# Bias strips from a table of ready rows, and new transfer estimates for a list scheduler, in a hybrid decoder step

## The chip, the core and the metric

The kernel runs on one core of one Trainium2 chip. The metric is the device time of one execution in microseconds. The time before is the median of three runs, 277.95 us (275.93, 277.95 and 278.9). A separate execution was profiled; its page and its trace are what is read here.

## The reference

One layer of a decoder trunk, for a new prompt of 512 tokens and for eight sequences that each add one token to a past. One projection of the 1024 wide input gives nine groups of columns; two mixers use them, and an output projection, a residual and a layer norm follow.

```python
h = jnp.einsum('btd,de->bte', x, w_in)
qa, ka, va, za, ga, qb, kb, vb, gb = jnp.split(h, split_points, axis=-1)
# mixer A: gated linear attention, 4 heads, dk 64, dv 128
log_a = jax.nn.log_sigmoid(einsum('btr,rk->btk', za, w_alpha2) + b_alpha) / 16
o_a, s_new = gla_chunked(qa * DK_A**-0.5, ka, va, log_a, s0, chunk=64)
o_a = o_a * rsqrt(mean(o_a**2) + eps) * gla_norm_g
# mixer B: 8 heads of 64; three (window, dilation) patterns: (128,1), (512,4), (2048,16)
logits = einsum('bqhd,bqjhd->bhqj', q, kg) * scale + rel_bias[t5_bucket(dist)]
# softmax over each pattern; the three outputs merged by their denominators
mix = concatenate([o_a * silu(ga), o_b * silu(gb)])
x_new = layer_norm(DEEPNORM_ALPHA * x + mix @ w_out, ln_g, ln_b)
```

Outputs are the new rows of the prompt and of the samples, both recurrent states, and the keys and values of both. All inputs and outputs are float32.

The three patterns share keys, so for a prompt the kernel adds them up: a key at distance d counts as often as patterns hold it, and the logarithm of that count is part of the bias. The bias depends on the distance alone. It is added to a tile of scores in which partition p holds the query p of a block and the columns hold keys; along the partitions the same sequence of biases is therefore shifted.

## The kernel before

Every product of the projections is made in three passes of fp32r (`three`): inputs and weights are split into a high and a low part, and hi x hi, lo x hi and hi x lo are added in PSUM. A feature group of 128 columns (`feature`) takes two banks of the class `d`, one for each half of the tokens (264 and 256 columns), with 24 matmuls each; after each an evacuation task is added that reads the bank on the vector engine (DVE) and the scalar engine (ACT). There are eight PSUM banks: three `d`, three `s`, two `t`.

Weights arrive as 512 KB transfers, are split by ACT (cast to the high part) and DVE (difference, the low part), and are taken in the fixed order of `ORDER`. The tasks of mixer A (levels `ps_l`, the diagonal `near`, the state), of mixer B and of the sample path run beside that.

Mixer B of a prompt goes by `scores(m, pi)`: m is one of four pairs of heads, pi one of two halves of the queries, so there are eight blocks. One block makes the scores of two heads and two query tiles in a batch of matmuls (`ps_s`). Then comes `softmax` for each head and tile: DVE adds the bias strip and takes the row extreme in one custom instruction (`tensor_tensor_reduce`, printed as ISA in the orders and as CUSTOM_DVE_ANT_0 in the trace) with a readout behind it; ACT takes the exponential with its sum; DVE inverts the sum; DVE or ACT scales; for the dilated part DVE transposes blocks of 32; PE transposes the probabilities (`ps_pt`), and DVE or ACT copies them to SBUF. `weighted` multiplies them with the values.

A **strip** is the bias tile of one head and one half: 128 partitions with 256 columns (pi = 0) or 320 (pi = 1). `bias_table` computes 768 biases for each of the 8 heads by two matmuls, writes them to DRAM (`tab`) and copies them within DRAM to `tabr`, where each of the 8 rows stands 35 times. Because a row is 768 long, a read with a step of 767 or 764 in place of 768 gives the shifted rows. `strips` reads each strip from there with an access pattern of 4 x 32 rows of 256; for pi = 1 a second transfer reads 64 more columns.

The **order of the work** is set by a planner (`Plan`). Every task is a generator that hands out its next instruction. Each step takes, over all tasks, the instruction that can begin earliest by estimated times, and among equals the lower priority number; matmuls of ordinary tasks count as ready only `SPARE` ns after their inputs. The order found is the program's order on each engine (PE, DVE, ACT, GpSimd as POOL, SyncE as SP, which issues nearly all transfers); on the chip each engine works strictly in that order. A step that gives two choices (`V.tensor_scalar(...), S.mul(...)`, or `copy`) takes the engine that would end first by the estimates. So the estimates decide the order and which engine copies, while the chip's own times decide how long it takes. The estimate of a transfer is in `Op.__init__`: bytes by a rate that is chosen from the run length and the outermost count, plus 600 ns for one class. A priority is the second argument of `add`.

All instructions are issued by one helper, so nearly every row of the profile has the line L377; rows are told apart by the names of their tiles.

Of the kernel before, what the change touches and what calls it, by code (L numbers as in the profile page):

```python
# [11 lines left out]
F32 = mybir.dt.float32  # L12
# [8 lines left out]
P = 128  # L21
# [9 lines left out]
HA, HB = 4, 8  # L31
# [23 lines left out]

T_N = 512
T_P = 768
T_R = 35
T_D = T_N + 128
T_W = T_D + 258  # L60

N_WARM = 7
ROWS = 66

SLOTS = dict(
    g=23,
    w=8, r=3,
    sv=4,
    pt=2, far=5, tp=2, vp=2,
    t2=2, st=3,  # L70
    pr=4,
    t1=5, ob=3,
    m=6)
BANKS = dict(d=3, s=3, t=2)


# [3 lines left out]
SWITCH = 140  # L80
RING = 8
PIECE = 256
SPARE = 800.0

ORDER = "qa0 qb0 qb1 qb2 qb3 kb0 kb1 vb0 kb2 kb3 gb0 vb1 gb1 gb2 va0 gb3 va1 ga0 ga1 ga2 ga3".split()

# [1 line left out]
class Op:  # L88
# [3 lines left out]
    def __init__(self, eng, fn, args, kw):  # L92
        self.eng, self.fn, self.args, self.kw = eng, fn, args, kw
        Op.made += 1
        aps = [x for x in args if isinstance(x, bass.AP)]
        extra = [x for x in kw.values() if isinstance(x, bass.AP)]
        self.writes, self.reads = [aps[0]], aps[1:] + [x for k, x in kw.items() if isinstance(x, bass.AP) and k != "accum_out"]
        if "accum_out" in kw:
            self.writes.append(kw["accum_out"])
        if fn == "tensor_tensor_reduce":  # L100
            self.writes.append(self.reads.pop())
        n = max(size(x) for x in aps + extra)
        psum = any(x.tensor.space == bass.MemoryType.PSUM for x in aps)
        self.mode = None
        self.port = eng.name == "POOL" or (eng.name == "DVE" and len(aps) + len(extra) > 1 and not psum and n > 64)
        if fn == "dma_start":
            c = 640 if eng.name == "SP" else 100
            x = aps[aps[0].tensor.space == bass.MemoryType.DRAM]
            run = 4 * min(run_of(x) for x in aps)

            rate = 130 if run <= 128 else 175 if x.ap[0][1] <= 64 else 340 if run >= 4096 else 230
            self.xfer = max(4 * total(x) / rate, 200)
            self.late = 600 * (rate == 175)
        elif eng.name == "PE":
            m, n, slow = size(aps[1]), size(aps[2]), aps[2].dtype == F32

            self.mode = tuple(32 if x <= 32 else 64 if x <= 64 else P for x in (aps[1].ap[0][1], m if slow and fn != "transpose" else P))
            r0 = aps[1].offset // aps[1].ap[0][0] // 32
            c0 = aps[0].offset // aps[0].ap[0][0] // 32 if self.mode[1] < P else 0
            self.cells = [(r, k) for r in range(r0, r0 + self.mode[0] // 32) for k in range(c0, c0 + self.mode[1] // 32)]  # L120
            self.gap = 17 if slow and fn != "transpose" else 5
            if fn == "transpose":
                c = 109
            else:
                c = 2 * max(n * .8333 + 2, m * .83 + 5) if slow else max(n, 64) * .4167 + 11
        elif eng.name == "DVE":
            fast = fn in ("tensor_copy", "tensor_scalar", "memset") and not psum
            ptr = fn in ("tensor_scalar", "scalar_tensor_tensor") and any(size(x) == 1 for x in aps[1:]) and n > 1
            c = ((n / 2 if fast else n) + (155 if fn == "transpose" else 124 if ptr else 66)) / .96
        elif eng.name == "ACT":  # L130
            c = n / 1.2 + (52 if psum else 97) + 90 * (len(extra) + (fn == "mul" and len(aps) > 2))
        else:
            c = n * .87 if fn == "memset" else n * 2.15 + 100
        self.cost = c


def run_of(x):

    n = 1
    for step, c in reversed(x.ap[1:]):  # L140
        if step != n:
            break
        n *= c
    return n


def size(x):
# [234 lines left out]
def trunk(ctx: ExitStack, tc: tile.TileContext, xT, xp, xs, state, ck, cv, w_in, wab, gnorm,  # L382
# [78 lines left out]
    o_pv, o_bs, o_as = cst("o_pv", [P, 4, NB]), vnt, cst("o_as", [P, NB * HA])  # L461
    yts = lt[:, 0, :].rearrange("p (m b) -> p m b", b=NB)
    ga_s, gb_s = cst("ga_s", [P, 4, NB]), cst("gb_s", [P, 4, NB])
    tabr = dram.tile([HB, T_R, T_P], F32, name="tabr")
    vad = dram.tile([NB, 512], F32, name="vad")
    qsd = dram.tile([NB, 512], F32, name="qsd")
    psd_s = dram.tile([64, 256], F32, name="psd_s")
# [215 lines left out]
    def feature(g, evac):  # L683

        yield At(g.name)
        for u in range(2):
            ps = yield bank("d", f"ps_{g.name}{u}")
            for k in range(KT):
                yield from three(ps[:, :TW[u]], k, halves(k, u, g))
            add(evac(ps, u), 2)  # L690
        g.done(0)

    def token(g, evac_f, evac):
# [87 lines left out]
    def dense():  # L781
# [25 lines left out]
                             start=k == 0, stop=k == KT - 1, skip_group_check=True)  # L807
                    for k in range(KT) for j in range(TT))
        free(zw, *xraw)
        add(gate_decay(pz), 24.7)  # L810
        yield from make("ka", Need("g", "ka", [P, 2, NP]), 3)
        yield from make("qa", Need("g", "qa", [P, 2, NP]), 2)
        for n in first:
# [62 lines left out]

    def bias_table():
        yield At("const")
        tab = dram.tile([HB, T_P], F32, name="tab")
        raw = yield Need("g", "ct_raw", [66, T_D])  # L880
        yield D.dma_start(raw, c_t[:, :T_D])
        ct = yield Need("g", "ct", [66, T_D], F32R)
        yield V.tensor_copy(ct, raw)
        free(raw)
        tsb = yield Need("g", "tsb", [HB, T_P])
        yield V.memset(tsb[:, T_N:T_P - P], NEG)
        yield At("rb")
        for c, to in ((slice(0, T_N), slice(0, T_N)), (slice(T_N, T_D), slice(T_P - P, T_P))):
            pt = yield bank("t", "ps_tab")
            yield T.matmul(pt[:HB, :c.stop - c.start], rb[:, 0, :], ct[:, c], start=True, stop=True)  # L890
            yield copy(tsb[:, to], pt[:HB, :c.stop - c.start])
            free(pt)
        yield D.dma_start(tab, tsb)
        free(ct, tsb)
        yield D.dma_start(tabr, tab[:, None, :].to_broadcast([HB, T_R, T_P]))
        mark("tab")


# [326 lines left out]
    def strips():  # L1225
        yield At("tab")
        yield At("qb", 1)
        for h0, pi in ((0, 0), (0, 1), (4, 0), (4, 1)):
            for h in range(h0, h0 + 4):
                yield At(f"kb{h // 2}{pi}")  # L1230
                strip = yield Need("st", f"strip{h}{pi}", [P, 256 + 64 * pi])
                plan.share(strip, 2)
                B["strip", h, pi] = strip
                row = tabr[h]
                yield D.dma_start(strip[:, 64 * pi:], bass.AP(tensor=row.tensor, offset=row.offset + T_N - P - 1, ap=[[T_P - 1, 4], [T_P - 4, 32], [1, 256]]))
                if pi:
                    yield D.dma_start(strip[:, :64], bass.AP(tensor=row.tensor, offset=row.offset + T_P - P + 31, ap=[[0, 4], [T_P - 1, 32], [1, 64]]))
                mark(f"strip{h}{pi}")

    def scores(m, pi):  # L1240
# [26 lines left out]
        for v in range(2):  # L1267
# [1 line left out]
                plan.share(ps[v, qt[0]], 2)  # L1269
                plan.share(pr[v, qt[0]], 2)  # L1270
            for q in qt:
                add(softmax(2 * m + v, q, ps[v, q], pr[v, q], cols[q]), 31 + m // 2 / 5 + pi / 10 + m % 2 / 50)

    def softmax(h, q, ps_all, pr_all, cols):
        ps, pr = ps_all[:, cols], pr_all[:, cols]
# [583 lines left out]
    add(sample_values(), 14.3)  # L1859
    add(sample_v(vnt, "vnt", by_tile(vw_s)), 21.3)  # L1860
    add(sample_v(vat, "vat", by_tile(vad)), 21.3)
    add(sample_past(), 19.3)
    add(sample_state(), 61)
    add(sample_gla(), 24.7)
    add(mix_sample_a(), 20.7)
    add(mix_sample_b(), 12.3)
    add(ln_rows(), 19.3)
# [5 lines left out]
    for pi in range(2):  # L1873
        for n in "ab":
            add(mix_tiles(n, pi), 12.7)
        for m in range(4):
            add(scores(m, pi), 31 + m // 2 / 5 + pi / 10 + m % 2 / 50)
        for g in range(2):
            add(weighted(g, pi), 30 + g / 5 + pi / 10)
        for j in range(2):  # L1880
# [104 lines left out]
```

## Time and profile before

| what | value |
| --- | --- |
| three timed runs | 275.93, 277.95, 278.9 us |
| span of the profiled execution | 275.6 us (its own time beside the span is not given) |
| PE busy | 266.9 us, 97%, 2881 instructions |
| DVE busy | 214.6 us, 78% |
| ACT busy | 158.5 us, 58% |
| POOL busy | 52.8 us, 19% |
| DMA | 52.58 MB, mean 191 GB/s |
| packets under 512 B | 13645 of 61527 |

The page gives each engine's busy time, the chain of work that ended last and the costliest groups. The waits of an engine list what it stood idle for and what released it. A table of windows gives the same by stretch. The timeline gives single instructions with their start and duration.

### The profile page before, as it was taken

What the parts mean: (1) busy time and instruction counts of PE and PEld (TensorE: products, weight loads), DVE (VectorE), ACT (ScalarE), POOL (GpSimd) and SP (SyncE); (2) the same over time, 40 slices, a digit from 0 to 9 for tenths busy, and PEclk for the clock granted to TensorE, in tenths of its full rate; (3) what the DMA queues carried; (4) which work ended last, traced back from release to release, by engine and by line L of the source; (5) the groups of instructions that cost most, each with busy time, mean ns of one, the idle gap of its engine ahead of it and who ended that gap; (6) DMA issues with size and microseconds to landing.
All of it is one profiled execution on the core that took longest, in us unless ns stands there. A gap on an engine that the chain in (4) does not pass through costs nothing.

```text
span 275.6 us, 7460 instructions
## 1 busy us (share of the span) xinstructions
PE 266.9 (97%) x2881; PEld 252.1 (91%) x2881; DVE 214.6 (78%) x578; ACT 158.5 (58%) x478; POOL 52.8 (19%) x71
## 2 busy tenths in 40 slices
PE   8999999999899999999999999999999999999990
PEld 5999999999899989989999999999999999998890
DVE  4845899998989497998396963738999999239984
ACT  4727886475538583877686824535668886224401
POOL 3000000000534260703000633744242000000000
PEclk9999999999999999999999999999999999999998
DMA  7977939436967898556497979893897660980432
GB/s 219 340 181 190 266 91 235 125 104 179 311 188 161 243 291 276 157 115 157 87 258 195 221 202 188 250 279 92 265 246 194 179 223 6 293 239 0 180 129 76
DMA packets 61527, 52.58 MB, mean 191 GB/s; under 512 B 13645, under 2 KB 53715, under 8 KB 61493
## 3 DMA queue, kind: packets, MB, share of 16 engines
q1 hardware_dynamic: 60917, 51.66, 67.2%
q8 instruction: 22, 0.36, 0.5%
q10 hardware_dynamic: 576, 0.46, 0.5%
q14 instruction: 12, 0.10, 0.1%
HBM read 46.02 MB, written 6.42 MB: 190 GB/s over the span
## 4 chain that ended last, share of the span: by engine, by line
PE 94%; DVE 4%; ACT 1%; issue 0%; DVEq 0%
PE ps_ga L377 9%; PE ps_gb L377 9%; PE ps_qb L377 9%; PE ps_yf L377 8%; PE ps_kb L377 8%; PE ps_y L377 7%; PE ps_qa L377 5%; PE ps_ka L377 4%; PE ps_vb_f L377 4%; PE ps_va_f L377 4%; PE ps_vb L377 4%; PE ps_va L377 4%; PE ps_pv L377 3%; PE ps_s L377 3%; PE ps_pt L377 2%; PE ps_oa L377 2%
## 5 line engine op out<-in xcount | busy, mean ns | idle before, releaser
L377 POOL TENSOR_TENSOR past<-past,qbc 128x256 f32<-128x256 f32 x32 | 24.0, 782 | 99.5 <-DMA qbc<-qsd 91.6
L377 POOL TENSOR_TENSOR vv<-vv,pb 128x256 f32<-128x256 f32 x32 | 26.5, 860 | 55.3 <-DMA pb<-psd_s 49.4
L377 ACT ACTIVATE pr<-pr,ms 128x128 f32<-128x128 f32 (+3 forms) x48 | 22.8, 493 | 6.7 <-DVE ms L377 6.5
L377 DVE CUSTOM_DVE_ANT_0 pr<-ps_s,strip 128x128 f32<-128x128 f32 (+3 forms) x32 | 11.8, 410 | 6.9 <-PE ps_s L377 6.0
L377 ACT COPY pt<-ps_pt 128x256 f32<-128x256 f32 (+1 forms) x27 | 9.3, 354 | 11.1 <-PE ps_pt L377 11.1
L377 ACT ACTIVATE sg<-sg 128x264 f32<-128x264 f32 (+1 forms) x32 | 13.4, 420 | 0.5
L377 PE MATMUL ps_ka<-xx,hi_ka 128*128 128x264 f32 (+1 forms) x64 | 12.8, 296 | 0.0
L377 PE MATMUL ps_pt<-cf,pr 128*128 128x128 f32 x56 | 11.0, 274 | 0.0
L377 PEld LDWEIGHTS ps_ka<-xx,hi_ka 128*128 128x128 f32 x64 | 10.4, 201 | 0.0
L377 DVE TENSOR_REDUCE lt<-past 128x8 f32<-128x512 f32 x16 | 10.4, 671 | 0.0
L377 ACT ACTIVATE d<-d 128x512 f32<-128x512 f32 x11 | 6.9, 648 | 5.8 <-DVE d L377 5.8
L377 DVE TENSOR_REDUCE o_pv<-vv 128x4 f32<-128x1024 f32 x8 | 9.7, 1210 | 0.0
L377 ACT COPY feat_y<-ps_yf 128x256 f32<-128x256 f32 x7 | 2.6, 373 | 11.2 <-PE ps_yf L377 11.2
L377 PE MATMUL ps_ka<-xx,lo_ka 128*128 128x264 f32 (+1 forms) x32 | 9.0, 293 | 0.0
L377 DVE SCALAR_TENSOR_TENSOR y<-y,ps_yt 128x256 f32<-128x256 f32 x8 | 3.0, 418 | 6.9 <-PE ps_yt L377 6.9
L377 DVE SCALAR_TENSOR_TENSOR s<-v,ka_s,s 128x128 f32<-128x128 f32 x16 | 5.1, 343 | 3.2 <-DMA v<-vad 1.9
L377 PE MATMUL ps_qa<-xx,hi_ka 128*128 128x264 f32 (+1 forms) x32 | 7.4, 310 | 0.0
L377 PEld LDWEIGHTS ps_pt<-cf,pr 128*128 128x128 f32 x56 | 6.9, 140 | 0.3 <-issue 0.2
L377 PE MATMUL ps_kb<-xx,hi_kb__744 128*128 128x264 f32 (+1 forms) x32 | 6.2, 293 | 0.9 <-DVE ms L377 0.9
L377 PE MATMUL ps_pv<-pt,v 128*64 128x128 f32 (+1 forms) x80 | 6.9, 318 | 0.0
L377 PE MATMUL ps_gb<-xx,hi_gb__1903 128*128 128x264 f32 (+1 forms) x32 | 6.8, 295 | 0.0
L377 ACT CAST xx<-x_raw 128x520 fp32r<-128x520 f32 (+2 forms) x10 | 5.3, 539 | 2.6 <-DMA x_raw<-in_xT_dram 2.3
(570 smaller groups left out, 1065.8 us busy)
## 6 DMA issues: line engine op xcount, KB each, us to landing
past<-in_ck_dram SPq DMA_DIRECT2D x8, 512.0 KB
vv<-in_cv_dram SPq DMA_DIRECT2D x8, 512.0 KB
pb<-psd_s SPq DMA_DIRECT2D x16, 256.0 KB
s<-in_state_dram SPq DMA_DIRECT2D x4, 512.0 KB
strip<-tabr SPq DMA_DIRECT2D x16, 128.0 KB
qbc<-qsd SPq DMA_DIRECT2D x8, 256.0 KB
y<-in_xp_dram SPq DMA_DIRECT2D x4, 512.0 KB
x_raw<-in_xT_dram SPq DMA_DIRECT2D x6, 260.0 KB
```

Source lines behind the costliest of these rows:

```text
L377: getattr(eng.eng, op.fn)(*op.args, **op.kw)
```

## The change

1. **The table.** `bias_table` writes four copies of the 640 entries per head that the shifted part needs (`tab`, rows of 644 seen from a step that shifts by one each copy) and four copies of the 128 entries of the dilated part (`tabf`). Two transfers within DRAM, 1024 rows each (256 and 64 columns), then write `tabx`: for each head 128 ready rows of 320.
2. **The strips.** Each strip is one transfer of 128 whole rows of 256 or 320 elements. There are 16 transfers where there were 24.
3. **The estimate of a transfer.** It is now the number of runs (cut at 4096 bytes) times a time per run, divided by k, the largest number up to 16 that divides the outermost count of both sides (`outer`). The 600 ns addition is gone.
4. **Other numbers of the planner.** `SPARE` goes from 800 to 640 ns, the constant of a DVE transpose from 155 to 92, and seven priorities change.

The computation is the same. The matmul instructions are the same in kind and count; their order, the order on the other engines and the engine of some copies change.

```diff
-T_R = 35
+T_M = T_P - P
+T_R = T_M + 4
+T_S = 320
...
-SPARE = 800.0
+SPARE = 640.0
...
-            rate = 130 if run <= 128 else 175 if x.ap[0][1] <= 64 else 340 if run >= 4096 else 230
-            self.xfer = max(4 * total(x) / rate, 200)
-            self.late = 600 * (rate == 175)
+            run = min(run, 4096)
+            k = max(j for j in range(1, 17) if all(outer(x) % j == 0 for x in aps))
+            self.xfer = 4 * total(x) / run * max(13, 8.4 + .0368 * run) / k
+            self.late = 0
...
-            c = ((n / 2 if fast else n) + (155 if fn == "transpose" else 124 if ptr else 66)) / .96
+            c = ((n / 2 if fast else n) + (92 if fn == "transpose" else 124 if ptr else 66)) / .96
...
+def outer(x):
+    return next((c for _, c in x.ap if c != 1), 1)
...
-    tabr = dram.tile([HB, T_R, T_P], F32, name="tabr")
+    tabx = dram.tile([HB, P, T_S], F32, name="tabx")
...
-            add(evac(ps, u), 2)
+            add(evac(ps, u), 34.7)
...
-        add(gate_decay(pz), 24.7)
+        add(gate_decay(pz), 14.6)
...
-        tab = dram.tile([HB, T_P], F32, name="tab")
+        tab = dram.tile([HB, 4 * (T_R - 1)], F32, name="tab")
+        tabf = dram.tile([HB, 4, P], F32, name="tabf")
...
-        yield D.dma_start(tab, tsb)
+        yield D.dma_start(bass.AP(tensor=tab.tensor, offset=tab.offset, ap=[[4 * (T_R - 1), HB], [T_R, 4], [1, T_M]]),
+                          tsb[:, None, :T_M].to_broadcast([HB, 4, T_M]))
+        yield D.dma_start(tabf, tsb[:, None, T_M:].to_broadcast([HB, 4, P]))
         free(ct, tsb)
-        yield D.dma_start(tabr, tab[:, None, :].to_broadcast([HB, T_R, T_P]))
+        for src, first, row, step, c, n in ((tab, T_N - P - 1, T_R - 1, -4, T_S - 256, 256), (tabf, 31, P, -1, 0, T_S - 256)):
+            yield D.dma_start(bass.AP(tensor=tabx.tensor, offset=tabx.offset + c, ap=[[32 * T_S, 4 * HB], [T_S, 32], [1, n]]),
+                              bass.AP(tensor=src.tensor, offset=src.offset + first, ap=[[row, 4 * HB], [step, 32], [1, n]]))
...
-                row = tabr[h]
-                yield D.dma_start(strip[:, 64 * pi:], bass.AP(tensor=row.tensor, offset=row.offset + T_N - P - 1, ap=[[T_P - 1, 4], [T_P - 4, 32], [1, 256]]))
-                if pi:
-                    yield D.dma_start(strip[:, :64], bass.AP(tensor=row.tensor, offset=row.offset + T_P - P + 31, ap=[[0, 4], [T_P - 1, 32], [1, 64]]))
+                yield D.dma_start(strip, tabx[h][:, T_S - 256 - 64 * pi:])
...
-                add(softmax(2 * m + v, q, ps[v, q], pr[v, q], cols[q]), 31 + m // 2 / 5 + pi / 10 + m % 2 / 50)
+                add(softmax(2 * m + v, q, ps[v, q], pr[v, q], cols[q]), 7.1 + m // 2 / 5 + pi / 10 + m % 2 / 50)
...
-    add(sample_past(), 19.3)
+    add(sample_past(), 1.9)
     add(sample_state(), 61)
-    add(sample_gla(), 24.7)
+    add(sample_gla(), 28.4)
...
-            add(scores(m, pi), 31 + m // 2 / 5 + pi / 10 + m % 2 / 50)
+            add(scores(m, pi), 2.8 + m // 2 / 5 + pi / 10 + m % 2 / 50)
```

How the order moves is shown at three places. First SP's queue around the first two strips, before (`raw_kb`, `raw_gb` and `raw_vb` are weights, `past` and `qbc` belong to the samples' past keys, numbers are buffer numbers):

```order
L377 DMA raw_gb__1071<-in_w_in_dram 128x8x128
L377 DMA qsd<-q_rows 4x8x128
L377 DMA past_1088<-in_ck_dram 128x1024
L377 DMA strip_1130<-tabr 128x1x256
L377 DMA strip_1132<-tabr 128x1x256
L377 DMA qbc_1096<-qsd 128x512
```

and after:

```order
L377 DMA qsd<-q_rows 4x8x128
L377 DMA past_1107<-in_ck_dram 128x1024
L377 DMA strip_1190<-tabx 128x256
L377 DMA strip_1193<-tabx 128x256
L377 DMA raw_gb__1111<-in_w_in_dram 128x8x128
L377 DMA qbc_1120<-qsd 128x512
```

The load of the gate weights moves from ahead of the sample's transfers and the strips to behind them.

Second DVE at the first scores (`kp` and `kw` are the keys, `near<-cm,ps_l` the mixer A levels, the ISA rows the bias add of the first head and its readout), before:

```order
L377 SCALAR_TENSOR_TENSOR kp_985<-ps_kb_1_1103,kp_985 128x256
L377 COPY_PREDICATED near<-cm,ps_l_1123 128x128x2
L377 STREAM_TRANSPOSE kw_1133<-ps_kb_1_1103 128x256
L377 ISA pr_1135,ms_1238<-ps_s_1137,strip_1130 128x128
L377 ISA ms_1238 128x1
L377 ISA pr_1135,ms_1239<-ps_s_1137,strip_1130 128x256
```

and after:

```order
L377 STREAM_TRANSPOSE kw_1191<-ps_kb_0_1059 128x256
L377 COPY_PREDICATED near<-cm,ps_l_1097 128x128x2
L377 COPY_PREDICATED near<-cm,ps_l_1097 128x256
L377 COPY_PREDICATED near<-cm,ps_l_1098 128x128x2
L377 COPY_PREDICATED near<-cm,ps_l_1098 128x256
L377 TENSOR_TENSOR qa<-eq,qa 128x448
L377 ISA pr_1196,ms_1214<-ps_s_1198,strip_1190 128x128
L377 ISA ms_1214 128x1
```

Four copies of the levels and a product of `qa` now stand ahead of the first bias add, where one copy stood before; the other three and the product came behind the bias adds. The scaling of the first probabilities, after:

```order
L377 RECIPROCAL ms_1214<-ms_1214 128x1
L377 TENSOR_TENSOR qa<-eq,qa 128x448
L377 TENSOR_SCALAR pr_1196<-pr_1196,ms_1214 128x128
L377 RECIPROCAL ms_1215<-ms_1215 128x1
L377 RECIPROCAL ms_1216<-ms_1216 128x1
L377 TENSOR_SCALAR pr_1196<-pr_1196,ms_1215 128x256
```

The second `qa` product stands between the first reciprocal and the first scaling; before, both `qa` products came behind all scalings of this block.

Third PE where the samples' state products (`ps_og`) and the first levels (`ps_l`) stand, before:

```order
L377 MATMUL ps_l_777<-qs,ks_347 64x32
L377 MATMUL ps_l_778<-qs,ks_347 64x32
L377 MATMUL ps_qb_1_781<-xx_259,hi_qb__493 128x256
L377 MATMUL ps_og<-s_705,qx 32x128 x8
L377 MATMUL ps_og<-s_707,qx 32x128 x8
L377 MATMUL ps_qb_1_781<-xx_258,lo_qb__494 128x256
```

and after:

```order
L377 MATMUL ps_qb_1_779<-xx_239,lo_qb__481 128x256
L377 MATMUL ps_og<-s_706,qx 32x128 x8
L377 MATMUL ps_og<-s_708,qx 32x128 x8
L377 MATMUL ps_l_796<-qs,ks_329 64x32
L377 MATMUL ps_l_797<-qs,ks_329 64x32
L377 MATMUL ps_l_796<-qs,ks_329 64x32
```

The state products came behind the levels, between projections; now they stand directly ahead of the levels.

More of the change, by code (lines that the diff above doesn't have):

```diff
@@ L63 @@
 ROWS = 66
[L65 to L73, printed above, removed]
+SLOTS = dict(g=23, w=8, r=3, sv=4, pt=2, far=5, tp=2, vp=2, t2=2, st=3, pr=4, t1=5, ob=3, m=6)
 BANKS = dict(d=3, s=3, t=2)
```

## The prediction

> **What bounds the kernel now.** I read the page first, then the waits of TensorE (PE), then a table of stretches.
>
> ```profile
> span 275.6 us, 7460 instructions
> PE 266.9 (97%) x2881; PEld 252.1 (91%) x2881; DVE 214.6 (78%) x578; ACT 158.5 (58%) x478; POOL 52.8 (19%) x71
> PE 94%; DVE 4%; ACT 1%; issue 0%; DVEq 0%
> PE warm_ps L377 <- DVE warm L1844: 1.2, 1, 1.2
> PE ps_kb L377 <- DVE ms L377: 0.9, 1, 0.9
> 45.00:67.00 22.00, 22.00 (x428) 21.32 (x427) 21.79 (x42) 13.34 (x37) 0.00 (x0) 1.00 0.50 138
> 67.00:75.00 8.00, 7.05 (x173) 6.53 (x172) 6.97 (x24) 5.03 (x16) 2.70 (x4) 1.00 0.95 288
> 75.00:100.00 25.00, 25.00 (x250) 23.74 (x248) 19.80 (x52) 15.01 (x44) 12.04 (x17) 1.00 0.81 212
> 100.00:150.00 50.00, 50.00 (x536) 46.29 (x533) 39.23 (x141) 35.09 (x107) 9.22 (x13) 1.00 0.68 185
> 266.00:276.00 10.00, 3.08 (x27) 2.88 (x25) 5.54 (x18) 1.06 (x4) 0.00 (x0) 0.87 0.16 56
> ```
>
> PE is busy for 266.9 of 275.6 us, and the chain that ended last is 94% PE. PE waits twice in the whole program: 1.2 us at the start and 0.9 us for `ps_kb`. In the table (stretch and its length, then busy time of PE, weight loads, DVE, ACT and POOL, clock, DMA share, GB/s) only 67 to 75 us has PE below its length, and there the DMA engines are 95% busy. So a change of order can win only what that stretch lost; the change leaves the first products and the last layer norm as they are (3.08 us of PE in the last stretch). The kernel is a full PE queue with one hole, and there is far more to lose than to win.
>
> The hole, in the timeline of PE (start, duration):
>
> ```profile
> 72.97 0.28 PE L377 MATMUL ps_kb<-xx,lo_kb__745 128*128 128x264 f32 x1
> 73.09 0.41 PE L377 MATMUL ps_kb<-xx,hi_kb__744 128*128 128x264 f32 x2
> 73.33 0.28 PE L377 MATMUL ps_kb<-xx,lo_kb__745 128*128 128x264 f32 x1
> 74.57 0.50 PE L377 MATMUL ps_kb<-xx,hi_kb__744 128*128 128x256 f32 x2 [0.95 <-DVE ms L377]
> 70.60 0.47 DVE L377 STREAM_TRANSPOSE kw<-ps_kb 128x256 f32<-128x256 f32 x1
> q8 instruction: 22, 0.36, 0.5%
> ```
>
> Products of this kind start 0.12 us apart (72.97 to 73.09); the one after 73.33 starts at 74.57, so 1.24 - 0.12 = 1.12 us are lost. The bank it writes had been read for the last time by the transpose at 70.60, which ended at 71.07, 3.5 us earlier. So the releaser named is not the cause. What is left is that PE had no instructions: code arrives by DMA too (queue q8: 22 packets, 0.36 MB, 16 KB each), and this is the stretch with the busiest DMA. That is an inference. [...]
>
> **The change, part by part.** *Strips and table.* These are the page's DMA rows, and SyncE's (SP) queue at the first strips:
>
> ```profile
> strip<-tabr SPq DMA_DIRECT2D x16, 128.0 KB
> tabr<-tab SPq DMA_DIRECT2D x1, 840.0 KB
> L377 SPq DMA_DIRECT2D tabr<-tab x1: 704/704/704, 25.0 to 25.0; - x1
> 63.12 0.37 SPq L377 DMA_DIRECT2D raw_gb__1071<-in_w_in_dram  x1
> 64.71 1.13 SPq L377 DMA_DIRECT2D strip<-tabr  x2
> 70.84 4.17 SPq L377 DMA_DIRECT2D strip<-tabr  x4
> L377 DVE CUSTOM_DVE_ANT_0 pr<-ps_s,strip 128x128 f32<-128x128 f32 x8 | 2.3, 286 | 0.9 <-DMA strip<-tabr 0.6
> ```
>
> 24 strip transfers become 16; SP saves 8 issues of 0.56 us (1.13/2), 4.5 us, and never sets the end. All waiting for strips in the program is 0.6 us, on DVE; PE is not behind it. The table costs one more write and one more DRAM copy, two issues of up to 0.7 us at about 25 us, and it is first read at 64.7, 40 us later. How long the new copies take is not in the trace; they would have to eat 40 us of cover before anyone waited, so I take nothing. The first strips now stand ahead of `raw_gb`, so that load starts about 1 us later; its first reader is the cast at 90.9:
>
> ```profile
> L377 ACT CAST hi_gb__1580<-raw_gb__1071 x1: 1052/1052/1052, 90.9 to 90.9; 128x1024 fp32r<-128x1024 f32 x1
> ```
>
> 27 us of cover, so nothing. [...]
>
> *The hole.* [...] Bounds: the hole goes (-1.1) or stays (0). I take -1.1, since in the whole trace it comes once, where queue and code demand coincide: 64 small products in 0.96 us, twice, just before it (rows below).
>
> *PE's order.* The multiset of PE instructions is unchanged. The order changes the tile mode 60 times instead of 62. A change of mode:
>
> ```profile
> 67.33 0.28 PE L377 MATMUL ps_kb<-xx,lo_kb__655 128*128 128x256 f32 x1
> 67.54 1.14 PE L377 MATMUL ps_l<-qs,ks 64*64 64x32 f32 x64
> 68.50 1.11 PE L377 MATMUL ps_l<-qs,ka 64*64 64x32 f32 x64
> 69.54 0.44 PE L377 MATMUL ps_s<-kp,qh 64*128 64x128 f32 x4
> 70.22 0.27 PE L377 MATMUL ps_s<-kp,ql 64*128 64x256 f32 x2
> 75.75 0.27 PE L377 MATMUL ps_pt<-cf,pr 128*128 128x128 f32 x1
> ```
>
> 0.21 us from 67.33 to 67.54 instead of 0.12: 0.09 each, -0.2 for two.
>
> *Scores, softmax and the near copies.* The scores' priority goes from 31 to 2.8 and softmax from 31 to 7.1. In the trace the first scores run from 69.54 to 70.49 and the first transpose of the probabilities starts at 75.75, 5.3 us later, of which the hole gave 1.1. What DVE did in between:
>
> ```profile
> 70.98 0.26 DVE L377 CUSTOM_DVE_ANT_0 pr<-ps_s,strip 128x128 f32<-128x128 f32 x1
> 72.25 0.16 DVE L377 RECIPROCAL ms<-ms 128x1 f32<-128x1 f32 x1
> 73.49 0.40 DVE L377 TENSOR_SCALAR pr<-pr,ms 128x256 f32<-128x256 f32 x1
> 74.38 1.00 DVE L377 TENSOR_SCALAR pr<-pr,ms 128x128 f32<-128x128 f32 x2
> 75.31 1.15 DVE L377 TENSOR_TENSOR qa<-eq,qa 128x448 f32<-128x448 f32 x1
> L377 DVE COPY_PREDICATED near<-cm,ps_l 128x256 f32<-128x256 uint8 x12 | 6.1, 536 | 0.1
> L377 ACT COPY pt<-ps_pt 128x256 f32<-128x256 f32 (+1 forms) x27 | 9.3, 354 | 11.1 <-PE ps_pt L377 11.1
> L377 DVE TENSOR_TENSOR gb<-ps_gb,sg 128x256 f32<-128x256 f32 x8 | 3.3, 416 | 2.3 <-ACT sg L377 2.3
> ```
>
> In the new order 39 products lie between the scores and the first transpose: 39 x 0.12 = 4.7 us. DVE now does four near copies (4 x 0.536 = 2.1) and one `qa` product (1.15) ahead of the scores' rows, 3.3 us from the end of the last `ps_l`; the scores end 9 x 0.12 + 0.95 = 2.0 us after that, so DVE starts 1.3 us late. Then come four bias adds with their readouts (70.98 to 72.25, 1.3), a reciprocal (0.16), the second `qa` (1.15) and the first scaling (0.5): 1.3 + 1.3 + 0.2 + 1.15 + 0.5 = 4.4 us, just inside 4.7. The next scaling ends 0.16 + 0.16 + 0.4 = 0.7 us later, at 5.1, and its transposes come 0.1 us after the first: about 0.3 us of waiting. DVE is 21.79 of 22 us busy in the stretch before, so it may be later still. Bounds: 0 to 2 us, the upper one if DVE is behind by the two `qa`; I take 0.6.
>
> *Copies and estimates.* By the new costs (transpose 92 for 155, SPARE 640 for 800) 13 copies out of PSUM go from ACT to DVE: 13 x 0.416 = 5.4 us more on DVE (80% of the span), less on ACT by 13 x 0.354 = 4.6. Its cover is DVE's idle time, 1.0 us in 67 to 75, 5.2 in 75 to 100 and 10.8 in 100 to 150; without cover it costs up to 5.4. SPARE, 160 ns less distance between a producer and PE, costs nothing while PE shows no wait for producers at all; at worst 0.16 us at each wait that appears. The feature evacuation, now after the softmax, holds one of the three `d` banks longer; another bank is filled meanwhile, 24 products x 0.12 = 2.9 us a bank.
>
> *Sample work.* `sample_past` comes first in its class. It is POOL products and DVE reductions off the chain:
>
> ```profile
> L377 POOL TENSOR_TENSOR past<-past,qbc 128x256 f32<-128x256 f32 x32 | 24.0, 782 | 99.5 <-DMA qbc<-qsd 91.6
> L377 DVE TENSOR_REDUCE lt<-past 128x8 f32<-128x512 f32 x16 | 10.4, 671 | 0.0
> ```
>
> Two products (1.6 us) come before each reduction; a reduction put too early on DVE would hold the evacuations behind it for up to 1.6 us. Inside the 5.8 us of two banks I take nothing. `gate_decay` and `sample_gla` move within the same cover.
>
> Sum on the profiled span: 275.6 - 1.1 - 0.2 + 0.6 = 274.9. The runs shown are 275.93, 277.95 and 278.9: the median lies 2.4 us above the span, the fastest 0.4. I apply the same -0.7 to the median: 277.2 us.
>
> **The rivals.** A measurement of this kernel can tell about 1%, 2.8 us, from no change.
>
> *Forecast, 0.52:* the hole goes, a part comes back at the first transposes. 277.2, its own range 276 to 279 by the bounds above.
>
> *The hole is not of that kind, or moves, 0.10.* Then -0.2 + 0.6 makes 278.4. For it: nothing in the views shows PE's instruction supply directly. Against: a bank that was free for 3.5 us. [...]
>
> *Faster by over 1%, 0.20.* [...]
>
> *Slower by over 1%, 0.18: softmax moves PE's wait to DVE.* There are eight blocks of scores, all earlier now, and DVE carries 5.4 us more. If DVE is behind at each, the transposes wait, and since PE works in order everything behind them does. Up to 0.6 us per block is 4.8 us: 277.95 - 1.3 + 4.8 = 281.5. It decides once DVE is more than 4.7 us behind the scores where it now is 4.4 to 5.1. For it: DVE at 21.79 of 22. Against: 16 us idle on DVE from 75 to 150.
>
> **How the numbers follow.** Likeliest 277.2. From 274.6 to 280.6 the range takes in the faster case, the forecast, the unmoved hole and the lower part of the slower case (three blocks late or more), and leaves out some 0.1 above it and some 0.05 below. Faster 0.20, within 1% 0.62 (0.52 + 0.10), slower 0.18.
>
> **What would show it.** Right: no PE gap of 1.1 us on a product of `ps_kb`, PE's waits listing `ps_pt` behind DVE `pr` at under a microsecond, DVE near 220 us busy, no wait for `strip`, the last product about 0.7 us earlier. Wrong: a wait of PE over 2 us in the scores' stretch, PE waiting for a `d` bank behind a feature evacuation, a clock below 1.00 after the start, or the DMA share of the hole's stretch unchanged and the hole still there.

## The result, and the profile after

The changed kernel is slower. Its median is 286.54 us (283.97 to 290.14) against 277.17 us for the kernel before (275.93 to 278.9); the ratio is 1.0305, 95% interval 1.0237 to 1.0373. A second group of runs gave 286.56 against 276.76 us, ratio 1.036 (1.030 to 1.042). The forecast was 277.2, range 274.6 to 280.6.

The execution of 290.14 us, which was the one profiled first, was a disturbed one, so the ratio of 1.0305 leaves it out and the rows below are from the profile of the same kernel in the second group (span 283.1 us, time 285.02). Time minus span is 1.7 to 3.3 us in the runs that list both, most often 2.0, so the span of 275.6 before stands for a time of about 277.6 us, near the median.

The page after, then the waits of PE, then the table of stretches (columns as before):

```profile
span 283.1 us, 7461 instructions
PE 267.6 (95%) x2881; PEld 251.3 (89%) x2881; DVE 213.9 (76%) x591; ACT 153.1 (54%) x465; POOL 55.1 (19%) x71
PE 51%; DMA 20%; DVE 11%; ACT 10%; SPq 4%; issue 2%; POOL 2%; DVEq 0%; ACTq 0%; POOLq 0%
...
PE ps_yt L377 <- ACT feat_y L377: 2.2, 1, 2.2
PE ps_dg L377 <- DVE dg L377: 1.4, 1, 1.4
PE warm_ps L377 <- DVE warm L1846: 1.2, 1, 1.2
PE ps_pt L377 <- DVE pr L377: 1.2, 1, 1.2
...
67.00:75.00 8.00, 7.36 (x175) 6.99 (x174) 6.10 (x13) 1.97 (x7) 0.00 (x0) 1.00 0.67 185
75.00:100.00 25.00, 23.82 (x238) 22.24 (x237) 21.41 (x76) 17.90 (x54) 13.66 (x16) 1.00 0.86 241
100.00:150.00 50.00, 49.16 (x497) 45.95 (x496) 39.73 (x132) 30.88 (x98) 16.72 (x21) 1.00 0.75 204
200.00:250.00 50.00, 47.83 (x535) 46.41 (x534) 39.62 (x130) 32.22 (x117) 0.00 (x0) 1.00 0.59 172
```

PE's busy time has hardly moved (266.9 to 267.6). What has grown is waiting: PE's listed waits add up to 9.0 us, where they were 2.1, and with the 0.7 us of busy time that is about the growth of the span (7.5 us). The chain that ended last was 94% PE and is now 51% PE and 20% DMA. In each of these stretches PE is busy for less than the length; before, that was so only in 67 to 75 (and in 200 to 250 it was busy for 50.00 of 50). DVE and ACT are no busier than before, so the time is not lost to work.

Three of these waits, each with what stood in front of it. The chain names the two weights (start of issue, time until they landed); the issue of the first two strips is in SP's rows (start, duration). The timeline gives the engine that stood behind each transfer and PE:

```profile
26.47 9.00 DMA raw_qb__444<-in_w_in_dram
229.24 10.95 DMA raw_wo__3762<-in_w_out_dram
68.67 0.91 SPq L377 DMA_DIRECT2D strip<-tabx  x2
...
36.63 1.23 DVE L377 TENSOR_TENSOR lo_qb__552<-raw_qb__444,hi_qb__551 128x1024 fp32r<-128x1024 f32 x1 [2.96 <-ACT hi_qb__551 L377]
39.80 0.68 DVE L377 TENSOR_REDUCE dg<-ps_dg 128x8 f32<-128x512 f32 x1
40.54 0.66 PE L377 MATMUL ps_dg<-cf,qk 128*128 128x128 f32 x4 [1.39 <-DVE dg L377]
75.03 0.29 DVE L377 CUSTOM_DVE_ANT_0 pr<-ps_s,strip 128x128 f32<-128x128 f32 x1 [1.57 <-DMA strip<-tabx]
77.08 0.33 PE L377 MATMUL ps_pt<-cf,pr 128*128 128x128 f32 x1 [1.18 <-DVE pr L377]
240.21 1.14 ACT L377 CAST hi_wo__3862<-raw_wo__3762 128x512 fp32r<-128x512 f32 x2 [4.87 <-DMA raw_wo__3762<-in_w_out_dram]
241.56 0.35 ACT L377 COPY feat_y<-ps_yf 128x256 f32<-128x256 f32 x1
241.96 0.44 PE L377 MATMUL ps_yt<-cf,feat_y 128*128 128x128 f32 x2 [2.17 <-ACT feat_y L377]
```

The pattern is the same each time. A weight or a strip lands late; DVE or ACT stands at the instruction that reads it (2.96, 1.57, 4.87 us), in order; what PE needs stands behind that instruction (the reduction `dg`, the scaled probabilities `pr`, the copy `feat_y`), and PE waits for that. The first case shows that the transfer need not be later than before. Weight `qb3` landed at 35.5 us (26.47 + 9.00). In the trace of before it was issued at 27.3 and cast at 36.7, no sooner. But there DVE did `dg` at 36.36 and the split of `qb3` at 39.33; now the split stands ahead of `dg`. The rows of before:

```profile
L377 SPq DMA_DIRECT2D raw_qb__472<-in_w_in_dram x1: 368/368/368, 27.3 to 27.3; - x1
L377 ACT CAST hi_qb__546<-raw_qb__472 x1: 1035/1035/1035, 36.7 to 36.7; 128x1024 fp32r<-128x1024 f32 x1
36.36 0.69 DVE L377 TENSOR_REDUCE dg<-ps_dg 128x8 f32<-128x512 f32 x1
39.33 1.22 DVE L377 TENSOR_TENSOR lo_qb__547<-raw_qb__472,hi_qb__546 128x1024 fp32r<-128x1024 f32 x1
```

Why the planner put it there shows in its own times beside those of the trace (landing in us; "plan" is the estimate by which the order was made):

```
                 before: plan  trace  late      after: plan  trace  late
weight qb3               37.9   35.0  -3.0            32.0   35.5   3.4
weight kb1               42.5   38.2  -4.2            35.5   38.7   3.2
first strip              70.1   69.8  -0.3            68.1   74.9   6.8
last output weight      223.3  226.9   3.6           224.4  240.2  15.8
```

The two weights land within 0.5 us of the same time in both kernels. The old plan counted on them 3 to 4 us after they were there, the new one 3 us before. The same holds for the time from issue to landing of all 33 weight loads after the first group: the median is 6.6 us in the old plan and 5.2 us in its trace, 3.3 us in the new plan and 5.7 us in its trace. The 15.8 us of the last weight are not one transfer's error. The plan had its issue at 216.5 us and the trace at 229.2, so 12.8 us had piled up by then.

### The profile page after: what moved, and what is told of

Read it like the earlier page. It is cut to its first block, busy times and chain, and to the rows that moved or that the text cites. A ratio compares the mean times of both kernels' runs of the same rounds, so it can differ in the third digit from the quotient of the medians.

```text
span 288.1 us, 7461 instructions
## 1 busy us (share of the span) xinstructions
PE 270.1 (94%) x2881; PEld 253.2 (88%) x2881; DVE 213.5 (74%) x591; ACT 153.2 (53%) x465; POOL 55.2 (19%) x71
## 4 chain that ended last, share of the span: by engine, by line
PE 34%; DMA 27%; DVE 13%; ACT 9%; SPq 7%; POOL 4%; issue 3%; POOLq 0%; DVEq 0%; ACTq 0%
SPq L377 7%; PE ps_y L377 7%; PE ps_qb L377 6%; DMA pb<-psd_s 5%; DMA raw_wo__3762<-in_w_out_dram 4%; PE ps_yf L377 4%; PE ps_gb L377 4%; DMA to_rows<-in_c_f_dram 4%; DMA strip<-tabx 3%; DMA raw_qb__444<-in_w_in_dram 3%; DMA qbc<-qsd 2%; PE ps_kb L377 2%; POOL vv L377 2%; PE ps_vb_f L377 2%; DMA past<-in_ck_dram 2%
## 5 line engine op out<-in xcount | busy, mean ns | idle before, releaser
L377 POOL TENSOR_TENSOR past<-past,qbc 128x256 f32<-128x256 f32 x32 | 26.5, 861 | 87.5 <-DMA qbc<-qsd 82.1
L377 ACT ACTIVATE pr<-pr,ms 128x288 f32<-128x288 f32 (+3 forms) x44 | 21.3, 493 | 19.7 <-DVE ms L377 19.6
L377 ACT COPY pt<-ps_pt 128x256 f32<-128x256 f32 (+1 forms) x26 | 8.4, 353 | 2.4 <-PE ps_pt L377 2.3
L377 ACT CAST mhb<-gb 128x256 fp32r<-128x256 f32 x8 | 3.3, 407 | 11.0 <-DVE gb L377 11.0
L377 PE MATMUL ps_yt<-cf,feat_y 128*128 128x128 f32 x16 | 3.6, 312 | 3.6 <-ACT feat_y L377 3.6
L377 DVE TENSOR_SCALAR pr<-pr,ms 128x256 f32<-128x256 f32 (+3 forms) x20 | 6.8, 358 | 0.1
```

The costliest lines, as they stand in the source:

```text
L377: getattr(eng.eng, op.fn)(*op.args, **op.kw)
```

## The experiments

The change has three parts: the **table** (with its strips), the **estimate** of transfers, and the **numbers** (priorities, SPARE, the transpose constant). Ratios are to the kernel before, run beside on the same chip. Theory A, at the start: the new order costs, not the new transfers. Theory B: the new table copies cost.

**The changed kernel again** (no edit).

> The changed kernel itself once more, beside the others of this group, so that they can be compared on one chip. Both theories: ratio 1.03 as measured, with the same gaps of TensorE at the same places: about 1.7 us where ps_dg waits near 39 us, 1 to 2 us at ps_kb, ps_va_f and ps_turn, and a gap of 2 to 4 us at the last weights of the output projection near 240 us. If the gap near 240 us is only an accident of one execution, it is under 1 us here and the ratio is nearer 1.01.

1.036 (1.030 to 1.042). The gaps are those shown above; the one near 240 us is there (2.2 us), so it is no accident. Of the others that were expected, those at `ps_dg` (1.4) and `ps_kb` (0.8) are there, and those at `ps_va_f` and `ps_turn` are not.

**The order of before with the new transfers.** The planner sees the old transfers; what is emitted in their places are the new ones:

```diff
-        getattr(eng.eng, op.fn)(*op.args, **op.kw)
+        for args in getattr(op, "emit", (op.args,)):
+            getattr(eng.eng, op.fn)(*args, **op.kw)
...
-        yield D.dma_start(strip[:, 64 * pi:], ...)
+        yield put(D.dma_start(strip[:, 64 * pi:], ...), (strip, tabx[h][:, T_S - 256 - 64 * pi:]))
```

> The order of before on every engine, word for word, with the new table and the one-transfer strips put where the old ones stood. Theory A (the new order is what costs): 0.99 to 1.005 of before; the strips land sooner, the hole at ps_kb near 73 us shrinks or goes. Theory B (the new table copies, 1.25 MB where there were 0.84, cost by themselves): 1.005 to 1.01, with a gap of 1 to 2 us near 39 us.

276.26 us, 0.998 (0.9963 to 0.9993). Theory B falls: at a fixed order the new table and strips cost nothing, they gain 0.5 us. The hole near 73 us is not in this trace (what that is worth as evidence comes with e16), and DVE waits for no strip. PE's waits, the stretch of the hole and the place itself:

```profile
PE warm_ps L386 <- DVE warm L1863: 1.2, 1, 1.2
67.00:75.00 8.00, 8.00 (x183) 7.69 (x182) 7.05 (x24) 5.00 (x17) 2.72 (x4) 1.00 0.91 284
73.37 0.29 PE L386 MATMUL ps_kb<-xx,lo_kb__750 128*128 128x264 f32 x1
73.50 0.40 PE L386 MATMUL ps_kb<-xx,hi_kb__749 128*128 128x256 f32 x2
```

**The order of after with the old transfers** (the same device the other way round: `put(D.dma_start(strip, tabx...), <the old one or two transfers>)`).

> The order of the changed kernel on TensorE, DVE, ACT and POOL, word for word, with the old table copy and the 24 old strip transfers put where the new ones stand. [...] Theory B: 1.6 us or more faster than the changed kernel (ratio 1.02 or less), since the table copy ahead of the weights is smaller.

294.49 us, 1.0645 (1.061 to 1.069), where the changed kernel has 1.036. The order costs, as Theory A has it, and within it the new transfers are worth 8 us. At this order DVE waits 7.1 us for the strips on the old path (first two rows), and 3.1 us on the new one. The longest wait of PE, 4.5 us, has another wait ahead of it: DVE stands at two reductions of the sample's past, for POOL, before it comes to the bias adds:

```profile
72.34 0.29 DVE L383 CUSTOM_DVE_ANT_0 pr<-ps_s,strip 128x128 f32<-128x128 f32 x1 [0.48 <-DMA strip<-tabr]
74.57 0.29 DVE L383 CUSTOM_DVE_ANT_0 pr<-ps_s,strip 128x128 f32<-128x128 f32 x1 [1.59 <-DMA strip<-tabr]
107.43 0.69 DVE L383 TENSOR_REDUCE lt<-past 128x8 f32<-128x512 f32 x1 [1.81 <-POOL past L383]
109.33 0.69 DVE L383 TENSOR_REDUCE lt<-past 128x8 f32<-128x512 f32 x1 [0.61 <-POOL past L383]
111.64 0.59 PE L383 MATMUL ps_kb<-xx,hi_kb__1388 128*128 128x264 f32 x2 [4.51 <-DVE ms L383]
```

**The numbers alone** (before, with the seven priorities, SPARE 640 and 92 for 155; nothing else).

> Before with the new priorities, SPARE 640 and the transpose constant alone; old table, old strips, old transfer estimate. If the priorities are the part of the change that costs: 1.02 to 1.04. If the transfer estimate is: 0.99 to 1.01.

285.42 us, 1.031 (1.027 to 1.034). It looked as if the priorities were the cause. DVE waits 4.9 us for strips here (0.6 before). Two theories were then set against each other: A1, the priorities cost; A2, whatever moves the order of before costs.

**Table and estimate, numbers as before.**

> Before with the new table, the one-transfer strips and the new transfer estimate, which change the order too; priorities, SPARE and the transpose constant as before. Theory A1 (the new priorities are what costs): 0.99 to 1.005, no gap of TensorE over 1 us. Theory A2 (the order of before is one good order among many, and whatever moves it costs): 1.015 to 1.04, with gaps at other places than in the changed kernel.

284.64 us, 1.030 (1.024 to 1.036). A1 falls.

**One group of numbers back, in the changed kernel.** Three runs, each with one edit:

```diff
-            add(evac(ps, u), 34.7)
+            add(evac(ps, u), 2)
...
-SPARE = 640.0
+SPARE = 800.0
...
-    add(sample_past(), 1.9)
+    add(sample_past(), 19.3)
```

With the first go the scores and the softmax back to 31, with the second the transpose constant back to 155, with the third `sample_gla` and `gate_decay` back to 24.7.

> The changed kernel with the old priorities of the scores, the softmax and the feature evacuation (31, 31, 2); all else as changed. A1, if these three are the part that costs: under 1.01. A2: 1.015 to 1.04.

> The changed kernel with SPARE 800 and the transpose constant 155 again; all else as changed. If too little distance between producers and TensorE is what costs: 1.01 or less, with fewer and shorter gaps at ps_pt and ps_dg. A2: 1.015 to 1.04. If the two numbers do nothing: as the changed kernel, 1.03.

> The changed kernel with the old priorities of sample_past, sample_gla and gate_decay (19.3, 24.7, 24.7); all else as changed. If the early reductions of the sample path hold DVE back: 1.01 or less. A2: 1.015 to 1.04. If they do nothing: as the changed kernel, 1.03.

1.043 (1.035 to 1.051), 1.037 (1.031 to 1.043) and 1.040 (1.035 to 1.045). No group brings the time back.

**Before, with the smallest steps of the planner's numbers.** SPARE 800 to 790; the wait after a transfer 500 to 520 ns.

> Before with SPARE 790 in place of 800 and nothing else: old table, strips, estimates and priorities. The number itself gives TensorE 10 ns less distance, which no gap could notice; it only makes the planner come to another order from an early point on (about 300 of 2170 rows on TensorE, 63 of 158 on SP read differently). Theory A2 (whatever moves the order of before costs): 1.01 to 1.04, with gaps at loads that come late. Against A2 (it is the content of the change that costs, and other orders are as good): 0.995 to 1.005.

> Before with the planner's wait after a transfer at 520 in place of 500 ns and nothing else; the order differs from about the middle of the program on (142 rows on TensorE, 13 on SP). A2: 1.005 to 1.03, less than for a change that moves the order from the start. Against A2: 0.995 to 1.005.

1.013 (1.009 to 1.017) and 0.9955 (0.993 to 0.998). Ten nanoseconds in one number, which no wait could notice, cost 1.3%: the order alone does that (PE's waits in e9: 1.8 us at `ps_yf`, 1.4 at `ps_kb`). But A2 as stated falls too, since the second order is better than that of before.

**Transfers moved on SP, the rest of the changed kernel's order untouched** (theory C: three gaps come from transfers that stand late on SP). A transfer named here is held back until another has been emitted:

```diff
+HOLD = ((("tabx",), "raw0_kb1"), (("raw0_kb3", "qsd", "past0"), "strip10"),
+        (("st_s", "out_3", "s51", "v41", "y0", "y1", "w_s"), "raw3_wo1"))
```

The first run has all three, the second the last one alone.

> The changed kernel with its order on TensorE, DVE, ACT and POOL word for word, and three things moved on SP alone: the two table copies behind the weights kb0 and kb1; the first two strips ahead of the weights kb3 and the sample's first transfers; the last two output weights ahead of the sample's state store, state load, residual rows and norm weights. Theory C (the gaps at ps_dg, at the first ps_pt and at ps_yt come from transfers that stand late in SP's queue): the gaps of 1.6, 1.3 and 2.3 us at these three places go, 4 to 6 us less than the changed kernel, ratio 1.01 to 1.02. If engines and not transfers are late there: under 1.5 us less, 1.03.

> The changed kernel with only the third of these moves: the last two output weights ahead of the sample's stores and loads on SP. Theory C: the gap of 2.3 us at ps_yt near 240 us goes and nothing of it comes back later, 2 to 3 us less than the changed kernel, ratio 1.02 to 1.03. If what is moved back (state, residual rows) is then late itself: no gain, a gap at ps_y or a longer end.

1.039 (1.032 to 1.046) and 1.041 (1.036 to 1.045): nothing gained. In e11 the wait at `ps_dg` is gone and what is left at `ps_pt` is 0.3 us at most, but others have grown; PE's waits there:

```profile
PE ps_kb L396 <- DVE ms L396: 1.7, 1, 1.7
PE ps_yt L396 <- DVE y L396: 1.7, 1, 1.7
PE ps_kv L396 <- DVE mlb L396: 1.6, 1, 1.6
```

At `ps_yt` the weight is now in time, and the sample's `v`, moved behind it, is what DVE stands at. In e12 PE waits 1.8 us at the same place for the same `y`. Theory C had the transfers right and the remedy wrong. The reading that I took from this: whichever reader stood too early in an engine's order blocked it here (1.7 us in e11, 1.8 in e12).

That made theory D: the plan takes data as usable too early, everywhere, and so places readers too early. Theory E: the new numbers make a worse order whatever is expected.

**Landings 2 us later in the plan.** The changed kernel (e13), and table and estimate without the new numbers (e14), each with

```diff
-TO_PE, FROM_PE, OTHER, AFTER_DMA, WITHIN = 600.0, 250.0, 150.0, 500.0, 120.0
+TO_PE, FROM_PE, OTHER, AFTER_DMA, WITHIN = 600.0, 250.0, 150.0, 2500.0, 120.0
```

> The changed kernel with one number of the planner changed: it takes data of a transfer as usable 2500 ns after its estimated landing, not 500. Theory D (the new estimate is too early, and the order has no slack against transfers that land late): 1.00 to 1.015, gaps behind transfers gone. Theory E (the new priorities make a worse order by themselves): 1.025 to 1.04.

> The new table, strips and transfer estimate with the old priorities, and the same 2500 ns; with 500 ns it was 1.030. Theory D: 0.99 to 1.01. Theory E has no cause here and expects 1.03 as with 500 ns, or another number above 1.015.

278.44 us, 1.007 (1.004 to 1.009), from 1.036; and 279.34 us, 1.009 (1.006 to 1.013), from 1.030. PE's waits in e13:

```profile
PE warm_ps L377 <- DVE warm L1846: 1.2, 1, 1.2
PE ps_pt L377 <- ACT kd L377: 0.8, 1, 0.8
PE ps_rows L377 <- DVE vat L377: 0.6, 1, 0.6
```

**Table and numbers with the old estimate.**

> The new table, strips, priorities, SPARE and transpose constant with the old transfer estimate, which expects transfers later. Theory D: 1.00 to 1.015, the estimate being the cause. Theory E: 1.025 to 1.04 as with the priorities alone (1.031).

277.79 us, 1.0036 (1.0014 to 1.0057). This is the changed kernel without the estimate: of 3.6% some 0.4% is left. What ACT waits for on weights, in the changed kernel (first three rows) and here (the last):

```profile
ACT hi_wo__3862 L377 <- DMA raw_wo__3762<-in_w_out_dram: 4.9, 1, 4.9
ACT hi_qa__321 L377 <- DMA raw_qa__258<-in_w_in_dram: 3.7, 1, 3.7
ACT hi_qb__551 L377 <- DMA raw_qb__444<-in_w_in_dram: 3.0, 1, 3.0
...
ACT hi_ka L371 <- DMA raw_ka<-in_w_in_dram: 1.8, 4, 0.5
```

With the old estimate ACT waits for no weight after the first group. Theory D holds for the changed kernel, and E falls for it, since e15 has all the new numbers.

**Both gains together**: the order of e10 with the new transfers in it.

> The order that the planner makes of before with 520 ns after a transfer (0.9955 with the old strips), and in it the new table and the one-transfer strips at the old ones' places (0.998 at the order of before). If the two gains are apart: 0.993. If both took away the same hole at ps_kb near 73 us: 0.995, and no gap of TensorE over 0.5 us in either.

276.0 us, 0.9967 (0.995 to 0.998). The gains don't add up. That both took away the hole near 73 us is not shown. The orders of e10 and of before part only at 96.8 us of the planner's time, and e10 has the old table and strips; yet its trace has no hole, with the DMA engines as busy (0.95). And e14, with the new strips, has a stop of this kind in the middle of a row of small products, at a DMA share of 0.30. The stretch of the hole in e10, then e14:

```profile
67.00:75.00 8.00, 8.00 (x184) 7.83 (x184) 7.05 (x23) 5.41 (x18) 2.89 (x4) 1.00 0.95 285
54.00:57.00 3.00, 0.84 (x61) 0.73 (x53) 3.00 (x8) 1.51 (x3) 0.00 (x0) 1.00 0.30 83
57.00 0.32 PE L377 MATMUL ps_l<-qs,ks 64*64 64x32 f32 x8 [2.16 <-issue]
```

The version is faster than the kernel before by less than 1%, as are e2 and e10; these three can't be told apart.

**The last two corners**: the estimate alone, the table alone.

> Before with the new transfer estimate alone: old table, old strips, old priorities. Theory D: 1.015 to 1.035, since the estimate lets the planner expect every weight sooner than it lands. If the estimate only costs together with the new table: 0.995 to 1.01.

> Before with the new table and the one-transfer strips alone, ordered by the planner with the old estimate and the old priorities. Theory D: 0.995 to 1.01. If new transfers cost as soon as the planner orders around them: 1.015 or more.

The estimate alone: 283.37 us, 1.022 (1.014 to 1.030), as D has it. The table alone: 288.84 us, 1.042 (1.036 to 1.048), against D. The cause there is another. Most of it is one place (8.6 us of waits, of 11.7 us by which it is longer), where the planner's own times already had holes of 2.2 and 6.6 us (at 215 and 219 us): it had left the last gates of both mixers so late that DVE is full while PE has nothing. PE's waits, two instructions and three stretches of e18:

```profile
PE ps_yf L371 <- ACT mhb L371: 5.9, 1, 5.9
PE ps_oat L371 <- DVE ga L371: 2.7, 1, 2.7
221.28 1.94 PE L371 MATMUL ps_oat<-cf,oa 128*128 128x128 f32 x8 [2.73 <-DVE ga L371]
229.08 0.59 PE L371 MATMUL ps_yf<-mhb,hi_wo__3179 128*128 128x264 f32 x1 [5.86 <-ACT mhb L371]
216.00:222.00 6.00, 3.27 (x27) 3.03 (x25) 5.93 (x23) 5.19 (x17) 2.44 (x4) 0.89 1.04 303
222.00:229.00 7.00, 1.22 (x6) 0.73 (x4) 7.00 (x16) 2.97 (x7) 0.35 (x1) 0.50 0.28 88
229.00:235.00 6.00, 5.92 (x28) 5.71 (x28) 4.21 (x13) 3.17 (x10) 0.00 (x0) 0.55 0.15 39
```

The corners of the three parts, planned anew each time: none 1, table 1.042, estimate 1.022, numbers 1.031, table and estimate 1.030, table and numbers 1.004, all 1.031 to 1.036; estimate and numbers were not run. The parts don't add up: each corner is another order.

Are e13 to e15 fast by the luck of their orders, then? The waits of ACT speak against it. Below are its waits for weights after the first group, in us, for every order that the planner made:

| estimate | kernels | ACT waits for weights | ratio |
| --- | --- | --- | --- |
| new | changed, e5, e6, e7, e8, e17 | 13.1, 12.4, 8.2, 10.8, 13.2, 8.5 | 1.036, 1.030, 1.043, 1.037, 1.040, 1.022 |
| new, 2 us later | e13, e14 | 3.9, 4.5 | 1.007, 1.009 |
| old | before, e4, e9, e10, e15, e18 | 0.0, 0.4, 0.0, 0.0, 0.0, 0.0 | 1, 1.031, 1.013, 0.9955, 1.004, 1.042 |

Each order from the new estimate as it stands makes ACT stand for weights, 8 us and more, and is slow. With the old one ACT hardly stands, but two orders (e4, e18) are slow by other waits. So the early estimate is a cause of its own, and luck of the order is a second one, of the same size.

## Why the prediction was wrong, step by step

- **What bounds the kernel: right, and more so than I used it.** PE, 97% busy before, had much to lose. The time was lost as waits; PE's busy time grew by 0.7 us only.
- **The hole at 73 us: no run shows the -1.1 us of the sum.** The changed kernel has no hole there, and neither has e2, with the new transfers in the order of before. But e10 has none either, with the old transfers and the same orders up to that place, and e14 has a longer one with the new strips at a DMA share of 0.30. Nor were the DMA engines much less busy there with the new strips (0.91 in e2, where it was 0.95). So one execution of before had the hole; that the old strips or busy DMA engines made it is not shown, nor that PE was out of instructions there. That it is absent here is luck, not a merit of the prediction.
- **The strips and the table, "nothing": right at a fixed order (e2, -0.5 us), and beside the point.** I counted the table's cover to its first reader, 40 us, and looked for the cover of one moved load, `raw_gb`. Both were covered. I did not ask what the new estimate would do to the order of the readers of every other load.
- **The step that failed is "Copies and estimates".** It prices the transpose constant and SPARE, by 13 copies that change engine and by 160 ns. The new estimate of transfers has no term in it at all: I put it at nothing, without a reason. I never set the planned landings beside the landings in the trace. With the old estimate the two weights of the table land 3 to 4 us before the plan counts on them; with the new one 3 us after. From issue to landing the new formula gives 3.3 us in the median where the trace has 5.7; the old one gave 6.6 for 5.2 and was wrong on the safe side. What the runs showed in place of nothing: ACT, which waited for no weight after the first group, waits 13.1 us for weights, and what PE needs stands behind. That step is worth about 3% (1.036 to 1.007 by 2 us more in the plan, to 1.004 by the old estimate).
- **Softmax: the wait came, for another reason.** I took 0.6 us, from 0 to 2, at the first `ps_pt` with DVE as the cause; it is 1.2 us. But DVE had been idle for 1.57 us before the bias add, for a strip: "no wait for `strip`" was wrong (3.1 us in all). The two `qa` products, on which I spent most of the working, did not decide it: the first was done before the strip landed, the second took 0.61 us, not 1.15, of the 1.7 us between the bias add and the scaling.
- **Sample work, "nothing": too little.** DVE, which waited 0.0 us for POOL at the reductions `lt` before, waits 3.8 us there now. Two of them (0.63 us each) stand ahead of the bias adds at 105.9 us, behind which PE waits 0.8 us for `ps_kb`.
- **The slower rival: right sign, wrong mechanism.** It wanted DVE overfull from its 5.4 us of extra copies and the softmax chains. The 13 copies did move (DVE x578 to x591), yet DVE is less busy than before (213.9 for 214.6). It waits, it doesn't work.
- **Faster, 0.20: nothing showed it.** The runs on record lay 0.4 to 3.3 us above the span of another execution. Where time and span are of one run, the difference is some 2 us (1.7 to 3.3) whatever the kernel; nothing was to be had there.
- **SPARE "costs nothing": not shown.** e7 gives no gain from putting it back, but that is one more order. e9 shows that 10 ns of it move the time by 1.3% by way of the order.
- **Chances.** I gave 0.18 to slower by reading one place where the order moved. The evidence that would have raised it was in the trace: the 9.4 us from issue to reader of a weight (27.3 to 36.7, above), and DVE's rows, which come in the program's order (`near` at 70.08, `kw` at 70.60, the first bias add at 70.98, as listed for the kernel before).

What stays open: what part of e4's 3.1% comes from the late strips, why e9's order is worse by 1.3% and e10's better by 0.45%, and what the hole at 73 us is. None was taken apart.

## What to carry to other kernels

Where a planner orders in-order engines by estimated times, an estimate that is early can be dearer than one that is late, as here. With the plan 3 us ahead of the landings ACT waited 13.1 us for weights, with what PE needed behind it, and the ratio was 1.036. With 2 us more in the plan it was 3.9 us and 1.007 (e13), with the old estimate 0.0 us and 1.004 (e15). Fit such an estimate to when data can be used in the trace under load, and set the planned landings beside the measured ones before judging by the size of a change. To price the parts of such a change, keep the order fixed and swap the instructions (e2, e3); planning anew for each part mixes it with the luck of the order, which here is worth up to 4% (e18).

## What the runs showed of the hardware

A low granted clock can outlast a wait of PE, as in e18. PE waits 2.7 us up to 221.28 and 5.9 us up to 229.08. The clock is 0.87 in 220 to 221 and 0.50 in 222 to 229, so it fell during the first of the two waits. It is still 0.50 in 230 to 234, where PE is busy all the time and has 19 products in 4 us; at 1.00 the row of e7 has 36 in 4 us (which products, the rows do not say). The length of a wait alone did not decide it. In e11 the clock is 0.50 in 107 to 110, after a wait of 1.7 us that ended at 105.6; in e7 it is 1.00 in 190 to 194, after a wait of 2.3 us that ended at 189.5. In the changed kernel, whose longest wait in 200 to 250 is 2.2 us, it stays at 1.00. What lowers the clock is not shown. Two rows of e18, one of e11 and one of e7:

```profile
220.00:221.00 1.00, 0.00 (x0) 0.00 (x0) 1.00 (x4) 0.62 (x3) 1.00 (x3) 0.87 1.05 426
230.00:234.00 4.00, 4.00 (x19) 4.00 (x20) 3.21 (x10) 2.17 (x8) 0.00 (x0) 0.50 0.00 0
107.00:110.00 3.00, 3.00 (x15) 3.00 (x14) 3.00 (x12) 2.95 (x11) 2.21 (x5) 0.50 0.88 264
190.00:194.00 4.00, 4.00 (x36) 4.00 (x35) 1.00 (x3) 2.19 (x8) 2.15 (x4) 1.00 1.05 241
```
